# FFN in-projection of a two-layer backbone: products that accumulate in PSUM on copies of other products' sums, and four VectorE combinations a tile instead of seven

## The chip, the core and the metric

One core of one Trainium2 chip runs the whole computation in one launch. The metric is device time in microseconds (us), from the first to the last instruction of the program. The engines are named as in the profile: PE is TensorE (matrix products, from SBUF into PSUM), PEld is its loading of weights, DVE is VectorE, ACT is ScalarE, POOL is GpSimd, SP issues most DMAs. PSUM has eight banks; a bank holds 512 fp32 numbers in each of 128 partitions.

## The reference, cut to what matters

A backbone of two layers works on 512 latent and 256 context tokens with 1024 features. A layer is an FFN, a token mixer (gMLP in layer 0, attention in layer 1), and a second FFN; each has an adaptive shift, scale and gate, and ends in a layer norm.

```python
def swiglu(h, w_in, w_out):
    g, u = jnp.split(h @ w_in, 2, axis=-1)
    return (jax.nn.silu(g) * u) @ w_out

def ffn_sublayer(x, shift, scale, gate, w_in, w_out, ln_g, ln_b):
    y = swiglu(modulate(x, shift, scale), w_in, w_out)
    return layer_norm(ALPHA * x + 0.5 * gate * y, ln_g, ln_b)
```

`w_in` is 1024 x 5632 (2816 columns for g and 2816 for u), everything is fp32. What the change touches is `h @ w_in` with the silu and the product behind it, in three of the four FFNs: the two of layer 0 and the first of layer 1, which all see latent and context tokens (768). The last FFN sees 512 latent tokens and is built otherwise.

## The kernel before, in words

**Precision.** An fp32 operand is held as two parts of type fp32r, hi (a ScalarE copy, `CAST` in the profile) and lo (source minus hi, a VectorE `TENSOR_TENSOR`). A product takes three matmuls: hi x hi, lo x hi, hi x lo.

**A tile of the in-projection.** A tile is 128 of the 2816 columns of g and the same 128 of u, for all 768 tokens: 22 tiles per FFN. The tokens fall into two halves of 384, the 1024 features into two halves of 512. That is a 2 x 2 by 2 x 2 block product (rows: g, u; columns: the two token halves), and it is done by Winograd's form of Strassen's scheme with seven block products instead of eight (`tile_strassen`, line 988). The seven combinations of the input, B11, T1, T2, B21, T3, T4, B22, are `comb` boxes that are made once per FFN; the seven matching combinations of weights are made for each tile. One block product (`product`, line 930) is 4 pieces of 128 features x 3 matmuls = 12 matmuls of 128 x 384 into one bank.

With the products named after the input's combination, in the kernel before:

- g1 = B11 + B21 (second product accumulated in the same bank b1), then silu on ScalarE;
- v = B11, then v += T2; w = v + T3; w += T1; c = v + T3 + T4. T4's product is accumulated on T3's bank b4 and B22's on T1's bank b3 (argument `go_on`), so that one VectorE addition takes both;
- the first token half of the result is silu(g1) x c, the second silu(v + T1 + B22) x w.

This makes seven VectorE operations a tile behind the products: `v+=b2`, `w=v+b4`, `w+=b3`, `c=v+b4`, `g*c`, `v+=b3`, `v*w`. In the profile, `q` (or `pieces`, `acc`, `zraw`) is the SBUF place of v, g, w and c, `ps` a PSUM bank, `stage`, `act` or `acts` where results go for the out-projection.

**The opening.** For the first 8 tiles (`OPENED`) B11 and B21 are run earlier, while the other combinations of the input are still being made (`opening`, `open_half`, `combine`): v (a copy of B11's sum) and g (the silu) then wait in `pieces`, `acc`, `zraw` and so on (`new_pieces`). These opened tiles have five products left, in the order T2, T3, T1, T4, B22. The other 14 have seven: B11, T2, T3, T1, B21, T4, B22.

**The order of the work.** In the openings and in-projections every engine runs its instructions in the order of the Python program (`Pinned`, line 65; `pin`). One product is one slot (`slot`, line 163): the twelve matmuls; then the low halves that are still owed to weights made in the last slot (`flush`); then up to two new weight units (`pump`, from the generator `units`, line 285, which makes the sums and differences of raw weights on VectorE and the hi copies on ScalarE; the low halves are put off to the next flush); then the work behind the product (`post`). So in ScalarE's and VectorE's queues the post of a product stands behind the weights that are made in the same slot. Eight weight units can live at once (`W_BUFS`), two `sums` buffers serve the weight combinations, and while the input's combinations are being made no more than three units are made ahead (`LEAD`).

**Banks.** `bank()` (line 120) takes a tile from one pool of eight buffers with a common tag; the pool decides which of its buffers it is. The gMLP takes its banks from there too: two a chunk for a projection (`project`, each bank 24 matmuls of 128 x 384, read by ScalarE's gelu into `su`), three a chunk for the spatial mixing (`spatial`, 128 x 256 matmuls), and one now and then for a transpose. So do the out-projections, in which six or eight banks collect sums over all weights.

**Places in time** (profiled execution): the in-projections of the three FFNs run from about 40 to 375, 1187 to 1519 and 1697 to 2029 us, where the openings end at about 90, 1230 and 1740; the gMLP's chunks run from 757 to 993 us. `L89` is the line at which `Pinned` issues an instruction, so nearly all instructions of these parts carry it, and they are told apart by the names of their tiles.

Of the kernel before, what the change touches and what calls it, by code (L numbers as in the profile page):

```python
# [13 lines left out]
P = 128  # L14
# [79 lines left out]
class Backbone:  # L94
# [68 lines left out]
    def slot(self, post, n=1, fills=0):  # L163

        self.flush()
        if self.combining is not None:
# [118 lines left out]
    def units(self, jobs):  # L285
        dve, w = self.dve, None
        for kind, srcs in jobs:
# [13 lines left out]
            dve.tensor_tensor(s1, u1, u2, ALU.add)  # L301
            dve.tensor_tensor(s2, s1, g1, ALU.subtract)  # L302
            yield self.unit_of(s2)
# [4 lines left out]
            yield self.unit_of(s1)  # L308
            g2 = self.take()
            if kind == "s":  # L310
                yield self.unit_of(g2)
            w = self.unit_of(u2)
            self.drop(1)
            yield w
            dve.tensor_tensor(s2, g2, s2, ALU.subtract)
            w = self.unit_of(s2)
# [326 lines left out]
    def combine(self):  # L643
# [41 lines left out]
        for name in ("T3", "T4") if begun else ("T3", "T1", "T4"):  # L685
            self.new_comb(name)
        sub(h1[0], h2[0], h1[0])
        sub(h1[1], h2[1], h1[1])
        high("T3", 0, h1[0])
        high("T3", 1, h1[1])  # L690
        yield
        sub(h1[2], h2[2], h1[2])
        high("T3", 2, h1[2])
        low("T3", 0, h1[0])
        if begun:
            low("T3", 1, h1[1])
            high("T4", 0, t4[0])
            yield
            low("T3", 2, h1[2])
            high("T4", 1, t4[1])  # L700
        else:
            high("T1", 0, t1[0])
            yield
            low("T3", 1, h1[1])
            low("T3", 2, h1[2])
            high("T1", 1, t1[1])
            high("T1", 2, t1[2])
# [3 lines left out]
            high("T4", 0, t4[0])  # L711
            high("T4", 1, t4[1])
            yield
            low("T1", 2, t1[2])
        low("T4", 0, t4[0])
        high("T4", 2, t4[2])
        self.new_comb("B22")
        high("B22", 0, h2[0])
# [3 lines left out]
        high("B22", 1, h2[1])  # L722
        high("B22", 2, h2[2])
        yield
        for n in range(HALF):
            low("B22", n, h2[n])
# [1332 lines left out]
```

## Time and profile before

| | |
|---|---|
| three runs | 2817.80, 2817.64, 2816.89 us (median 2817.64) |
| profiled execution, span from first to last instruction | 2816.9 us |
| mean granted TensorE clock | 0.998 |
| PE busy | 2771.2 us (98%), 14478 matmuls |
| DVE busy | 2101.1 us (75%), 3681 instructions |
| ACT busy | 1163.0 us (41%), 2245 instructions |
| POOL busy | 537.4 us (19%) |
| in-projection matmuls `ps<-comb,w` (128 x 384) | 5544, idle before them 9.8 us in all |

How to read the views: a row of the grouped view is "line engine operation out<-in shapes xcount | busy, mean ns | idle time before, and what ended most of it". In a timeline a row is "start, duration, engine, ...", a run of like instructions is drawn together as xN, and [x <-ENGINE tile] is idle time before it and what ended that. A matmul is drawn from its start to its modelled end, and the next one starts before that end. A window's row gives for each engine the busy time and the number of instructions, then the granted clock as a share of the full one, the DMA share and GB/s.

### The profile page before, as it was taken

To read this page: it belongs to the slowest core of one execution; us is meant where nothing else is said; L and a number is where in the kernel's file an instruction comes from. 1 tells how busy PE (TensorE), PEld (TensorE's weight loads), DVE (VectorE), ACT (ScalarE), POOL (GpSimd) and SP (SyncE) were. 2 spreads that over 40 slices of the span, in tenths; PEclk is the share of its full clock that TensorE was granted. 3 is DMA by queue.
4 is the path that set the end of the run, shared out by engine and by line. 5 is a ranking of instruction groups with operands and counts; after the bars stand their busy time and mean duration, and the time that the engine had idled before them with its cause. 6 is when DMAs were issued, how large, how long until landed. Compare 5 with 4: busy or idle time off the path is not lost.

```text
span 2816.9 us, 40812 instructions
## 1 busy us (share of the span) xinstructions
PE 2771.2 (98%) x14478; PEld 2501.4 (89%) x14478; DVE 2101.1 (75%) x3681; ACT 1163.0 (41%) x2245; POOL 537.4 (19%) x605
## 2 busy tenths in 40 slices
PE   7999999999999999999999999999999999999998
PEld 5999988888899988899999889999988888888886
DVE  6988879587687776698888759888886598733445
ACT  6433432442355532463334236333432666623321
POOL 1001044333321232200102220000242121000001
PEclk9999999999999999999999999999999999999999
DMA  7443366366565474344336534434595524454352
GB/s 232 131 135 122 112 225 211 114 199 198 184 180 167 150 237 140 123 148 139 121 121 200 181 113 133 144 120 124 154 314 152 148 69 88 132 150 132 113 168 82
DMA packets 398819, 429.99 MB, mean 153 GB/s; under 512 B 28504, under 2 KB 288024, under 8 KB 398616
## 3 DMA queue, kind: packets, MB, share of 16 engines
q1 hardware_dynamic: 364504, 319.40, 37.0%
q0 software_dynamic: 34112, 108.00, 12.4%
q8 instruction: 113, 1.85, 0.3%
q14 instruction: 90, 0.74, 0.1%
HBM read 366.10 MB, written 63.41 MB: 152 GB/s over the span
## 4 chain that ended last, share of the span: by engine, by line
PE 86%; DVE 5%; issue 3%; ACT 3%; DMA 1%; POOL 1%; SPq 0%; DVEq 0%; POOLq 0%; ACTq 0%
PE ps L89 86%; DVE w L89 1%; DMA raw<-in_w_mod_dram 1%; PE pp L89 1%; POOL acc L383 0%; POOL rs L184 0%; ACT z L1957 0%; DMA raw<-in_ffn_w_in_dram 0%; DVE comb L89 0%; DVE w L156 0%; ACT h L601 0%; ACT p L1473 0%; ACT w L155 0%; ACT w L89 0%; DVE nm L1465 0%
## 5 line engine op out<-in xcount | busy, mean ns | idle before, releaser
L89 PE MATMUL ps<-comb,w 128*128 128x384 f32 x5544 | 972.2, 335 | 9.8 <-DVE q L89 2.6
L89 PEld LDWEIGHTS ps<-comb,w 128*128 128x128 f32 x5544 | 961.1, 188 | 16.8 <-DVE w L89 3.8
L89 PE MATMUL ps<-w,acts 128*128 128x512 f32 (+1 forms) x3792 | 860.1, 388 | 0.0
L89 PEld LDWEIGHTS ps<-w,acts 128*128 128x128 f32 x3792 | 707.3, 188 | 145.0
L89 ACT CAST w<-raw 128x512 fp32r<-128x512 f32 x630 | 387.7, 620 | 819.9 <-PE ps L89 723.2
L89 DVE TENSOR_TENSOR w<-raw,w 128x512 fp32r<-128x512 f32 x630 | 454.8, 729 | 260.0 <-ACT w L89 259.9
L89 PE MATMUL ps<-h,w 128*128 128x384 f32 (+2 forms) x2304 | 445.1, 353 | 0.2 <-DVE w L156 0.2
L89 PEld LDWEIGHTS ps<-h,w 128*128 128x128 f32 x2304 | 402.4, 188 | 37.8 <-DVE w L156 0.4
L89 DVE SCALAR_TENSOR_TENSOR acc<-mraw,cs,acc 128x512 f32<-128x512 f32 x378 | 279.2, 772 | 20.3 <-DMA mraw<-in_w_mod_dram 19.8
L89 PE MATMUL ps<-w,h 128*128 128x512 f32 x1200 | 274.6, 390 | 0.0
L383 POOL PARTITION_ALL_REDUCE acc<-acc x56 | 204.8, 3660 | 351.4 <-DVE acc L89 331.3
L89 PEld LDWEIGHTS ps<-w,h 128*128 128x128 f32 x1200 | 224.6, 188 | 46.3
L89 POOL DMA_DIRECT2D act<-stage x84 | 48.4, 576 | 973.5 <-DVE stage L89 934.6
L89 DVE TENSOR_TENSOR q<-q,ps 128x384 f32<-128x384 f32 (+1 forms) x258 | 143.7, 557 | 106.5 <-PE ps L89 89.3
L89 ACT CAST w<-sums 128x512 fp32r<-128x512 f32 x198 | 122.8, 620 | 237.8 <-DVE sums L302 118.1
L89 POOL DMA_DIRECT2D q<-act x226 | 129.0, 625 | 466.1 <-DVE acts L89 308.4
L89 ACT CAST acts<-q 128x384 fp32r<-128x384 f32 (+1 forms) x262 | 127.3, 519 | 78.9 <-DVE q L89 44.2
L89 DVE TENSOR_TENSOR acts<-q,acts 128x384 fp32r<-128x384 f32 (+1 forms) x262 | 145.5, 588 | 8.3 <-ACT acts L89 8.3
L89 DVE TENSOR_TENSOR w<-sums,w 128x512 fp32r<-128x512 f32 x198 | 140.2, 708 | 1.9 <-ACT w L89 1.9
L156 DVE TENSOR_TENSOR w<-raw,w 128x512 fp32r<-128x512 f32 x114 | 75.8, 688 | 28.8 <-ACT w L155 28.4
L184 POOL TENSOR_TENSOR rs<-ve,mhalf 128x1 f32<-128x1 f32 (+3 forms) x47 | 39.1, 831 | 274.8 <-DVE ve L181 167.7
L155 ACT CAST w<-raw 128x512 fp32r<-128x512 f32 x114 | 68.1, 627 | 48.3 <-PE ps L89 25.5
(203 smaller groups left out, 2162.4 us busy)
## 6 DMA issues: line engine op xcount, KB each, us to landing
raw<-in_ffn_w_in_dram SPq DMA_DIRECT2D x400, 256.0 KB, 3.0
mraw<-in_w_mod_dram SPq DMA_DIRECT2D x256, 256.0 KB, 3.5
raw<-in_ffn_w_out_dram SPq DMA_DIRECT2D x176, 256.0 KB, 3.4
q<-act POOLq DMA_DIRECT2D x216, 192.0 KB, 4.3
act<-stage POOLq DMA_DIRECT2D x74, 384.0 KB, 2.9
raw<-in_gmlp_w_in_dram SPq DMA_DIRECT2D x96, 256.0 KB, 3.3
zhat<-z POOLq DMA_DIRECT2D x26, 512.0 KB, 2.9
raw<-in_gmlp_w_out_dram SPq DMA_DIRECT2D x48, 256.0 KB, 2.9
```

The costliest lines, as they stand in the source:

```text
L89: return self.tc.keep_in_program_order(f(*args, **kwargs))
L155: self.act.copy(hi, src)
L156: self.lows.append((key, lambda: self.dve.tensor_tensor(lo, src, hi.bitcast(F32), ALU.subtract)))
L184: self.last_rstd = self.nc.gpsimd.tensor_tensor(rs, ve, self.mhalf[:, 0:1].to_broadcast([P, n]), ALU.pow).ins
L383: nc.gpsimd.partition_all_reduce(accs[c], accs[c], P, bass_isa.ReduceOp.add)
```

## The change

The matmuls stay the same in number and shape. A block product now accumulates on a bank that already holds what has to be added to it:

- `seeded` is a bank into which ScalarE writes B11's sum: from b1 in a tile with seven products, from v in SBUF in an opened tile. T2's product accumulates on it; ScalarE copies the bank out to v. T3's product accumulates on the same bank; ScalarE copies it out to w. T4's product accumulates on it too, and VectorE multiplies g by the bank itself.
- T1's product goes to bank b2, and ScalarE copies it to p5. B22's product accumulates on b2.
- VectorE is left with four operations: `v += b2`, `w += p5`, `g * seeded`, `v * w`.

The order of the products becomes B11, T1, T2, B21, T3, B22, T4, and T2, T1, T3, B22, T4 in an opened tile. `units` yields the weights in that order, and `combine` makes T1, T3, B22, T4 in that order. `slot` gets `early`, work that stands ahead of the slot's new weights; the seed of a tile with seven products and ScalarE's copies out of T1's, T2's and T3's banks are put there. In an opened tile the seed is copied between the previous tile's last slot and T2's product.

An accumulating matmul on a bank that a copy has written needs a bank that matmuls have already written whole. `bank()` therefore chooses itself among eight tags with one buffer each: the one that was handed out longest ago and isn't held (`hold`, `unhold`), and for `seeded` one whose last user wrote all of the 384 columns (`marked`). This holds for every caller of `bank()` outside the attention, the gMLP included; the out-projections hold their banks until they are read. v and g of opened tile 7 lie in `acc` and no longer in `mraw`.

```diff
-    def bank(self):
-        return self.psum.tile([P, 512], F32, tag="ps", name="ps")
+    def bank(self, hold=None, whole=False, marked=False):
+        if self.pairs:
+            return self.psum.tile([P, 512], F32, tag="ps", name="ps")
+        held = self.bank_held.values()
+        x = next(x for x in self.bank_order if x not in held and (not marked or x in self.bank_whole))
+        self.bank_order.remove(x)
+        self.bank_order.append(x)
...
+        (self.bank_whole.add if whole else self.bank_whole.discard)(x)
+        return self.psum.tile([P, 512], F32, tag=f"ps{x}", bufs=1, name="ps")
...
-    def slot(self, post, n=1, fills=0):
+    def slot(self, post, n=1, fills=0, early=None):
         self.flush()
+        if early:
+            early()
         if self.combining is not None:
...
-        def step(ps, name, post, go_on=False, fills=0):
+        def step(ps, name, go_on, early=None, post=nothing, fills=0):
             self.product(ps, name, go_on)
-            self.slot(post, 2, fills)
+            self.slot(post, 2, fills, early)
             self.release(1)
         add = lambda out, a, b: dve.tensor_tensor(out, a, b, ALU.add)
+        seeded = self.part_bank(marked=True)
         if opened is None:
             b1, v = self.part_bank(), temp()
-            step(b1, "B11", lambda: act.copy(v, b1))
+            step(b1, "B11", False, lambda: act.copy(seeded, b1))
         else:
             v, g = opened
-        b2, b3, b4 = self.part_bank(), self.part_bank(), self.part_bank()
-        step(b2, "T2", lambda: add(v, v, b2))
-        w = temp()
-        step(b4, "T3", lambda: add(w, v, b4), fills=fills)
-        step(b3, "T1", lambda: add(w, w, b3))
+            act.copy(seeded, v)
+        b2, p5, w = self.part_bank(), temp(), temp()
+        keep5 = b2, "T1", False, lambda: act.copy(p5, b2)
+        keep6 = seeded, "T2", True, lambda: act.copy(v, seeded)
         if opened is None:
+            step(*keep5)
+            step(*keep6, fills=fills)
             g = temp()
-            step(b1, "B21", lambda: act.activation(g, b1, AF.Silu), True, int(fills > 1))
-        c = temp()
+            step(b1, "B21", True, None, lambda: act.activation(g, b1, AF.Silu), int(fills > 1))
+        else:
+            step(*keep6)
+            step(*keep5)
+        step(seeded, "T3", True, lambda: act.copy(w, seeded))
+
+        def second():
+            add(v, v, b2)
+            act.activation(v, v, AF.Silu)
+            add(w, w, p5)
+
+        step(b2, "B22", True, None, second)
...
-        def first():
-            add(c, v, b4)
+        def last():
             to = g if m is None else m[:, T1]
-            dve.tensor_tensor(to, g, c, ALU.mult)
+            dve.tensor_tensor(to, g, seeded, ALU.mult)
             done(T1, to)
-
-        step(b4, "T4", first, True)
-
-        def second():
-            add(v, v, b3)
-            act.activation(v, v, AF.Silu)
             to = v if m is None else m[:, T2]
             dve.tensor_tensor(to, v, w, ALU.mult)
             done(T2, to)
-        step(b3, "B22", second, True)
+        step(seeded, "T4", True, None, last)
```

**ScalarE, from one opened tile to the next.** The first rows are ScalarE's queue in the kernel before, in the second FFN, around the silu of its second opened tile (`pieces_11429` is that tile's v; `sums` and `raw` are the sources of weight units).

```order
L89 CAST w_12070<-sums_12067 128x512
L89 CAST w_12088<-raw_11944 128x512
L89 ACTIVATE pieces_11429<-pieces_11429 128x384
L89 CAST w_12114<-sums_12066 128x512
L89 CAST w_12131<-raw_11987 128x512
```

The same place in the changed kernel (`pieces_11415` is v of the second opened tile, `pieces_11477` that of the third, `ps_12079` the third tile's seeded bank):

```order
L89 CAST w_12056<-sums_12053 128x512
L89 ACTIVATE pieces_11415<-pieces_11415 128x384
L89 CAST w_12074<-sums_12052 128x512
L89 COPY ps_12079<-pieces_11477 128x384
L89 COPY pieces_11477<-ps_12079 128x384
L89 CAST w_12099<-raw_11945 128x512
```

The copy into the bank now stands behind the silu and one weight cast of the tile before it; the copy out, behind it, belongs to T2's product.

**VectorE and ScalarE at the first opened tile.** VectorE's queue in the changed kernel, in the second FFN, from the weights that are made in the first tile's T3 and B22 slots to that tile's `v += b2` (`pieces_11415<-pieces_11415,ps_11854`):

```order
L89 TENSOR_TENSOR w_11900<-sums_11894,w_11900 128x512
L339 TENSOR_TENSOR sums_11895<-raw_11828,sums_11895 128x512
L89 TENSOR_TENSOR w_11918<-raw_11758,w_11918 128x512
L320 TENSOR_TENSOR sums_11948<-raw_11877,raw_11920 128x512
L89 TENSOR_TENSOR w_11925<-sums_11895,w_11925 128x512
L89 TENSOR_TENSOR w_11943<-raw_11826,w_11943 128x512
L323 TENSOR_TENSOR sums_11949<-sums_11948,raw_11873 128x512
L89 TENSOR_TENSOR pieces_11415<-pieces_11415,ps_11854 128x384
```

And ScalarE's queue there, from the copy of T3's bank to w (`q_11856<-ps_11852`) to the seed of the second opened tile:

```order
L89 COPY q_11856<-ps_11852 128x384
L89 CAST w_11918<-raw_11758 128x512
L89 CAST w_11925<-sums_11895 128x512
L89 CAST w_11943<-raw_11826 128x512
L89 CAST w_11952<-sums_11949 128x512
L89 ACTIVATE pieces_11415<-pieces_11415 128x384
L89 CAST w_11971<-sums_11948 128x512
L89 COPY ps_11976<-pieces_11415 128x384
```

The addition to v stands behind the weight operations of the seven rows above it on VectorE; the silu that needs it stands behind four casts, and the next seed behind the silu and a cast. (Here the next tile's v is drawn under the same name, since it is another part of the same tile.)

**TensorE in the gMLP.** The matmuls between the projections of the first chunks in the changed kernel; they are the same and in the same order as before, and only the banks differ:

```order
L89 MATMUL ps_7317<-w_sT_7014,vn_7162 128x256 x4
L89 MATMUL ps_7322<-w_sT_7014,vn_7162 128x256 x4
L89 MATMUL ps_7327<-w_sT_7014,vn_7162 128x256 x4
L89 MATMUL ps_7365<-ident_69,s512_7140 128x128
L89 MATMUL ps_7370<-w_sT_7014,vn_7162 128x256 x4
L89 MATMUL ps_7375<-w_sT_7014,vn_7162 128x256 x4
L89 MATMUL ps_7380<-w_sT_7014,vn_7162 128x256 x4
```

Ahead of them stand the four projection banks of chunks 0 and 1, ps_7217, ps_7218, ps_7267 and ps_7268. With the bank that was handed out longest ago, ps_7370, ps_7375 and ps_7380 are the banks of ps_7217, ps_7218 and ps_7267.

More of the change, by code (lines that the diff above doesn't have):

```diff
@@ L684, in combine @@
                 yield
-        for name in ("T3", "T4") if begun else ("T3", "T1", "T4"):
+        for name in ("T3",) if begun else ("T1", "T3"):
             self.new_comb(name)
[L687 to L701, printed above, removed]
+        if not begun:
             high("T1", 0, t1[0])
-            yield
-            low("T3", 1, h1[1])
-            low("T3", 2, h1[2])
             high("T1", 1, t1[1])
-            high("T1", 2, t1[2])
             yield
@@ L721, in combine @@
         low("T4", 2, t4[2])
[L722 to L726, printed above, removed]
     def norm_stats(self, st):
@@ L869, in out_proj_latent @@
                     if not x:
-                        banks[b, half] = self.bank()
+                        banks[b, half] = self.bank(("out", b, half))
                     self.products(banks[b, half], b, [acts.of(order[x])], ws[half : half + 1], x == 0, False)
@@ L974, in new_pieces @@
             self.pieces += [self.zplace()[:, 0:HT] for _ in range(2)]
-        elif f == 7:
-            self.pieces += [
-                self.main.tile([P, 512], F32, tag="mraw", bufs=MRAW_BUFS, name="pieces")[:, 0:HT] for _ in range(2)
-            ]
     def opening(self, seq):
```

81 lines of the change are left out of this document (62 added, 19 removed).

## The prediction

> **What bounds the kernel now.** I read the page's busy times first, then the windows over one in-projection, then TensorE's waits and its timeline at the places where it waited.
>
> ```profile
> span 2816.9 us, 40812 instructions
> ...
> PE 2771.2 (98%) x14478; PEld 2501.4 (89%) x14478; DVE 2101.1 (75%) x3681; ACT 1163.0 (41%) x2245; POOL 537.4 (19%) x605
> ```
>
> TensorE is busy for all but 45.7 us of the span. The columns of the next view are PE, PEld, DVE, ACT, POOL, the granted clock and DMA.
>
> ```profile
> 1225.00:1240.00 15.00, 14.22 (x81) 13.64 (x81) 14.79 (x26) 8.11 (x16) 0.00 (x0) 1.00 0.43 125
> 1240.00:1385.00 145.00, 145.00 (x836) 144.60 (x835) 126.85 (x223) 52.59 (x93) 7.60 (x14) 1.00 0.45 137
> 1385.00:1400.00 15.00, 14.52 (x84) 14.20 (x83) 14.66 (x19) 5.18 (x10) 9.03 (x5) 1.00 0.34 96
> ```
>
> In the long window of the third sublayer's in-projection TensorE has no idle time: 145.00 us for 836 matmuls is 173.4 ns each, 2.08 us for a product of 12. The change leaves that number of matmuls alone, so VectorE work saved there is worth nothing by itself. VectorE is full (14.79 of 15, 14.66 of 15) only at the first tile and near one later tile. What it costs TensorE there is in its waits, cut here to the time from 60 to 2030 us:
>
> ```profile
> PE ps L89 <- DVE q L89: 2.6, 5, 0.5
> ...
> PE ps L89 <- ACT w L89: 1.4, 3, 0.9
> ```
>
> ```profile
> 79.75 11.89 PE L89 MATMUL ps<-comb,w 128*128 128x384 f32 x66
> 92.51 2.32 PE L89 MATMUL ps<-comb,w 128*128 128x384 f32 x12 [0.87 <-ACT w L89]
> 95.38 104.86 PE L89 MATMUL ps<-comb,w 128*128 128x384 f32 x603 [0.55 <-DVE q L89]
> ```
>
> ```profile
> 1208.78 27.32 PE L89 MATMUL ps<-comb,w 128*128 128x384 f32 x156
> 1236.33 1.97 PE L89 MATMUL ps<-comb,w 128*128 128x384 f32 x10 [0.23 <-ACT w L89]
> ```
>
> ```profile
> 1236.33 2.33 PE L89 MATMUL ps<-comb,w 128*128 128x384 f32 x12 [0.23 <-ACT w L89]
> ...
> 1398.50 1.68 PE L89 MATMUL ps<-comb,w 128*128 128x384 f32 x8 [0.48 <-DVE q L89]
> ```
>
> ```profile
> L89 PE MATMUL ps<-comb,w 128*128 128x384 f32 x5544 | 972.2, 335 | 9.8 <-DVE q L89 2.6 <-DVE w L89 2.6 <-ACT w L155 2.3
> ```
>
> A matmul's end is shown 335 ns after its start while the next is due after 173, so an idle time of x is a delay of x + 0.16. The 12 matmuls behind a wait take 2.33 us, not 12 x 0.1734 + 0.16 = 2.24: 0.09 more. The eight waits of the first view come to 2.6 + 1.4 + 8 x 0.25 = 6.0 us. Another 0.4 us goes at 83.04, where a product waits for ScalarE's late copy out of its bank.
>
> ```profile
> 83.04 8.27 PEld L89 LDWEIGHTS ps<-comb,w 128*128 128x128 f32 x48 [0.33 <-ACT pieces L89]
> ```
>
> So **6.4 us is all that relieving VectorE can give back.** The waits of "DVE w" lie in the openings, whose weights do not change.
>
> **The change, part by part.**
>
> *Matmuls and combinations.* 7 products a tile before and after. Three of seven combinations go, 3 x 66 x 0.55 us = 109 us of VectorE, which lies beside a TensorE that never pauses, but for those 6.4 us.
>
> ```profile
> L89 DVE TENSOR_TENSOR q<-q,ps 128x384 f32<-128x384 f32 x246 | 135.4, 551 | 57.3 <-PE ps L89 40.1 <-ACT w L89 12.2
> ```
>
> ```profile
> L89 ACT CAST acts<-q 128x384 fp32r<-128x384 f32 x240 | 114.0, 510 | 77.4 <-DVE q L89 44.1 <-DMA q<-act 32.8
> ...
> L89 ACT ACTIVATE q<-q 128x384 f32<-128x384 f32 x45 | 23.7, 526 | 88.0 <-DVE q L89 88.0
> ...
> L89 ACT COPY q<-ps 128x384 f32<-128x384 f32 x44 | 21.0, 478 | 10.4 <-PE ps L89 10.4
> ```
>
> *ScalarE copies.* The three that empty T1's, T2's and T3's banks take 0.48 us each, and one product (2.08 us) stands between each and the matmul that needs the bank. That product hides them; without it each would hold TensorE some 0.6 us. In the 14 unopened tiles the seed is copied after B11 with T1 in between: hidden too. No copy from SBUF into PSUM is in the trace; it lies between 0.48 (out of PSUM) and 0.53 (SBUF to SBUF). I take 0.51, the row that also reads SBUF.
>
> The Trainium skill (PSUM — Partial Sum Buffer, Specifications) says that ScalarE writes PSUM faster than SBUF; no row here shows it. With 0.48 for a seed the sum below would be 0.6 us smaller.
>
> *The seed of the opened tiles* is the wait that the change adds: v already lies in SBUF, and T2, which accumulates on the seed, directly follows the previous tile's T4. On ScalarE the seed stands behind that tile's silu and a weight cast, and the silu behind VectorE's v + B22. The rows of one tile now, where B22 is the last product and the addition was released by TensorE:
>
> ```profile
> 1813.79 0.55 DVE L89 TENSOR_TENSOR zraw<-zraw,ps 128x384 f32<-128x384 f32 x1 [0.33 <-PE ps L89]
> 1814.37 0.53 ACT L89 ACTIVATE zraw<-zraw 128x384 f32<-128x384 f32 x1 [2.00 <-DVE zraw L89]
> 1814.81 0.61 ACT L89 CAST w<-raw 128x512 fp32r<-128x512 f32 x1
> ```
>
> ```profile
> 1235.62 0.61 ACT L89 CAST w<-raw 128x512 fp32r<-128x512 f32 x1
> ...
> 1236.14 0.61 ACT L89 CAST w<-sums 128x512 fp32r<-128x512 f32 x1
> ```
>
> From the addition's start: silu at 0.58, cast at 1.02, next ScalarE instruction 0.52 later (second fence) at 1.54, seed done at 2.05, TensorE 0.10 after that (the cast of 1235.62 ends at 1236.23, the matmul starts at 1236.33): 2.15. T2 is due 12 matmuls after T4 started, and T4 started 0.20 before the addition: 1.88. So 0.27 + 0.09 = **0.36 us for a tile that follows an opened one**, from 0.1 (a short seed, a quick start) to 0.6 (the addition held up). In a third of the tiles it now starts up to 0.1 later, but then VectorE had more to do. There are 7 such places in each of 3 sublayers. At 18 of them, 6.5 us; the first of each is worse.
>
> *The first opened tile.* Its seed stands behind the opening's last silu. In the second FFN (1200 to 1519 us), T2 was due three products before 1236.10 - 0.16, at 1229.70. The last opening product ends at 1229.86, silu 0.04 later, the next ScalarE instruction 0.38 on (half of the row below), seed 0.51, start 0.10: 1230.89, so 1.2 + 0.09 = 1.3 us. The first FFN has a comb cast in between (0.52): 1.8 + 0.09 = 1.9. Bounds 1.0 and 2.5 each: ScalarE was at most some tenths late there.
>
> *The step from the first to the second opened tile.* Two weights a slot are still made ahead there. I walk the new order with 0.60 us for a 512-wide VectorE operation (two in 1.28 below), 0.52 for a cast, 0.04 from one engine to the next, t = 0 at T2's start; the products end at 2.33, 4.41, 6.49, 8.57.
>
> ```profile
> 1215.33 1.28 DVE L89 TENSOR_TENSOR z<-z 128x512 f32<-128x512 f32 x2
> ```
>
> ScalarE copies T2 at 2.4 and casts B22's and T4's weights at 2.7 and 3.3; VectorE's low halves of these follow at 3.4 and 4.0, the next tile's s2 at 4.6. ScalarE casts it and s1 at 5.3 and 5.9, copies T3 at 6.5, casts u1 at 6.9. VectorE: two low halves and g2 - s2, 6.0 to 7.9, cast at 7.9 and 8.45 with u2; then u1's low half, an s1, two low halves and an s2, 7.8 to 10.9. **Only then comes v + B22, at 10.8, though B22's sum was there at 8.6.** ScalarE casts that s2 at 10.9; silu 11.45, cast 11.9, seed 12.4 to 12.9, T2 at 13.0, due at 10.49: 2.5 + 0.09 = 2.6 us. The third FFN has the same order. In the first, a further cast stands ahead of the silu and one behind it; the two behind wait for sums that VectorE makes only after the addition, so the same walk gives T2 at 14.0, 3.6 us. Bounds 1.5 and 4.0. In the second tile one weight a slot is made, the addition is free by 8.6, and the 0.36 holds.
>
> *Banks in the gMLP.* bank() now takes the bank that was handed out longest ago, also there. The third mixing bank of chunk 1 is the eighth after the first half of chunk 1's projection, which ScalarE has not yet read. TensorE reaches it after 8 of the 12 matmuls of 774.76, at 775.9; the gelu that frees it runs at 776.98.
>
> ```profile
> 774.76 1.91 PE L89 MATMUL ps<-w_sT,vn 128*128 128x256 f32 x12
> ```
>
> ```profile
> 776.98 0.87 ACT L89 ACTIVATE su<-ps 128x384 f32<-128x384 f32 x2
> ```
>
> It ends at 777.47: 0.10 later TensorE goes on, 1.6 + 0.09 = 1.7 us, once; from nothing (ScalarE earlier) to 2.5.
>
> *The rest:* holds in the out-projections hand banks out in the order of before; T4's combination comes later, but its low halves are through before the tile's T4; tile 7's acc places are free before the first fill of tile 8. Nothing.
>
> **The sum.** First FFN 1.9 + 3.6 + 6 x 0.36 = 7.7; second and third 1.3 + 2.6 + 2.2 = 6.1 each; gMLP 1.7: 21.6 us of new waits, less the 6.4 that go: +15.2. On the profiled span 2816.9, which lies 0.7 under the median 2817.64 of the runs, that is 2832.1; I say **2832 us, slower by 0.5%**. With all terms at their low ends 1.8 + 4.5 + 3.0 - 6.4 = +2.9, at the high ones 10.8 + 12 + 7.5 + 2.5 - 5 = +28.
>
> **The rivals.**
>
> *Hidden seeds.* If ScalarE reaches the steady seeds in time, because PSUM is nearer or the addition starts sooner, their 6.5 us go: 2826. For it: only 0.27 us are missing. Against: every hop is a row. 12%.
>
> *All of the cover holds (the other side).* VectorE's relief also pulls in the first two seeds and the gelu; nothing is left but the eight waits and the late copy: 2816.9 - 6.4 = 2810.5, faster by 0.2%. It decides if the first tile's silu runs before the casts of the next weights. For it: VectorE is full just there. Against: the casts stand ahead of it in the order. 4%.
>
> *A balance.* Weights are ready earlier than walked, the first steps cost 1.5 and no bank waits: 3 x 1.5 + 4.5 + 18 x 0.2 - 6.4 = +6 at most, 2817 to 2823: 8%.
>
> *The clock falls.* TensorE pauses 2.6 and 3.6 us in one piece, longer than any wait in the FFNs now. Early in the kernel the clock did fall, after a broken stretch, and not after a wait of 1.89 us:
>
> ```profile
> 30.00:40.00 10.00, 6.53 (x40) 4.09 (x38) 7.67 (x20) 6.79 (x13) 0.00 (x0) 1.00 0.97 312
> 40.00:50.00 10.00, 9.30 (x56) 7.35 (x56) 6.44 (x13) 8.39 (x21) 0.00 (x0) 0.83 0.67 208
> 50.00:60.00 10.00, 8.00 (x46) 7.14 (x46) 7.91 (x17) 8.16 (x17) 0.00 (x0) 1.00 0.81 226
> ```
>
> ```profile
> 40.70 3.76 PE L89 MATMUL ps<-comb,w 128*128 128x384 f32 x12
> ...
> 51.51 0.62 PE L89 MATMUL ps<-comb,w 128*128 128x384 f32 x2 [1.89 <-ACT w L155]
> ```
>
> The product at 40.70 took 3.76 instead of 2.24. Three times 1.5 us: 2832 + 4.6 = 2837. 12%.
>
> The Trainium skill (TensorE: Matmul & The Clock Gate, What's actually happening) puts the drop behind an idle window of about 3.4 us; by that rule only the wait in the first FFN could reach it, 2833.5. The 1.89 us without a drop agree.
>
> **How the numbers follow.** Forecast 64%, its own range 2826 to 2838 from the bounds of the first steps and the seeds; the rivals 12, 4, 8 and 12%. The range 2823 to 2840 leaves out the fast side, most of the balance, and a few per cent above. Slower by over 0.2% (some 5.6 us, about what a measurement can tell from no change): forecast, hidden seeds and falling clock, 88%; within it the balance, 8%; faster 4%.
>
> **What would show it.** In the profile after, TensorE's waits in the FFNs name ScalarE's writes into ps (a COPY ps<-pieces and its like), some 24 of them: 18 near 0.1 to 0.3 us of idle time, one of 2 to 3.5 us in each FFN a tile after the opening, one of 1 to 2 us at its end. The waits for "DVE q" and "ACT w" near 92, 1236 and 1398 are gone, VectorE is some 100 us less busy, ScalarE as much more. A wait of TensorE for gelu stands near 785. No wait at the opened tiles would make the seeds' chain wrong; waits of 1 us there would say that the addition is held up in every tile; a TensorE whose matmul spacing changes would make all of it wrong.

## The result

The changed kernel takes **2835.75 us** (median of 4 runs, 2835.25 to 2836.71) where the kernel before took 2817.72 (4 runs, 2816.89 to 2818.25): ratio **1.0064**, 95% interval 1.0050 to 1.0079. It is slower by 18.0 us; 2832 with 2823 to 2840 was forecast.

The profile of the changed kernel, with the lines that answer to those shown of before: its page (span, busy time of the engines),

```profile
span 2834.9 us, 40738 instructions
...
PE 2781.4 (98%) x14478; PEld 2508.5 (88%) x14478; DVE 2012.9 (71%) x3483; ACT 1245.0 (44%) x2467; POOL 537.6 (19%) x605
```

TensorE's waits from 60 to 2050 us (engine and tile that wait, engine and tile that end the wait; us in all, times, longest),

```profile
PE ps L89 <- ACT ps L89: 12.6, 6, 3.3
PE ps L89 <- DVE w L89: 2.5, 4, 0.7
PE ps L89 <- ACT su L89: 1.4, 1, 1.4
```

and its timeline at the first tiles of the first and the second FFN:

```profile
85.03 10.70 PE L89 MATMUL ps<-comb,w 128*128 128x384 f32 x60 [1.73 <-ACT ps L89]
99.00 11.20 PE L89 MATMUL ps<-comb,w 128*128 128x384 f32 x48 [3.27 <-ACT ps L89]
```

```profile
1238.53 10.69 PE L89 MATMUL ps<-comb,w 128*128 128x384 f32 x60 [1.19 <-ACT ps L89]
1251.85 78.41 PE L89 MATMUL ps<-comb,w 128*128 128x384 f32 x432 [2.63 <-ACT ps L89]
```

VectorE is 88 us less busy (some 100 was forecast), ScalarE 82 more, and the waits for "DVE q" and "ACT w" are gone. In their place stand six long waits for a seed, two in each FFN. The 18 short ones lie below what the first view lists: their idle time is 0.01 each, but the start of the matmul comes 0.17 late and the next one 0.11.

To see where the 18 us came from, I compared the start of the same matmul in the two traces, stage by stage:

| part | after minus before, us |
|---|---|
| start of the program, to 70 us | -1.8 |
| first FFN's in-projection | +7.9 |
| gMLP, chunk 1 | +1.4 |
| in-projection at 1200 to 1519 us | +5.5 |
| in-projection at 1710 to 2029 us | +5.5 |
| the rest | -0.4 |
| sum | 18.1 |

The start of the program differs by up to 3.2 us between the profiled executions of all kernels below, the change's -1.8 among them, so I compare places in the traces behind it rather than single times (of the experiments only `seed_early` and `best` have more than one run). Behind it the change is 19.9 us later, the seeds, the clock and the bank together, less what VectorE's relief gives back.

### The profile page after: what moved, and what is told of

It reads as the page before. It is cut to its first block, busy times and chain, and to the rows that moved or that the text cites. A ratio compares the mean times of both kernels' runs of the same rounds, so it can differ in the third digit from the quotient of the medians.

```text
span 2834.9 us, 40738 instructions
## 1 busy us (share of the span) xinstructions
PE 2781.4 (98%) x14478; PEld 2508.5 (88%) x14478; DVE 2012.9 (71%) x3483; ACT 1245.0 (44%) x2467; POOL 537.6 (19%) x605
## 4 chain that ended last, share of the span: by engine, by line
PE 63%; ACT 3%; DVE 3%; issue 2%; POOL 1%; DMA 0%; DVEq 0%; POOLq 0%; ACTq 0%; SPq 0%
PE ps L89 62%; PE pp L89 1%; POOL acc L410 0%; ACT z L1991 0%; DVE z L89 0%; POOL rs L203 0%; ACT h L628 0%; DVE comb L89 0%; ACT w L89 0%; ACT p L1507 0%; DVE w L89 0%; DMA raw<-in_ffn_w_in_dram 0%; DVE nm L1499 0%; ACT w L172 0%; ACT comb L642 0%
## 5 line engine op out<-in xcount | busy, mean ns | idle before, releaser
L89 PE MATMUL ps<-comb,w 128*128 128x384 f32 x5544 | 982.8, 337 | 17.6 <-ACT ps L89 12.6
L89 PEld LDWEIGHTS ps<-comb,w 128*128 128x128 f32 x5544 | 967.8, 189 | 28.2 <-ACT ps L89 20.7
L89 PE MATMUL ps<-w,acts 128*128 128x512 f32 (+1 forms) x3792 | 860.1, 388 | 0.0
L89 PEld LDWEIGHTS ps<-w,acts 128*128 128x128 f32 x3792 | 707.6, 188 | 144.7
L89 ACT CAST w<-raw 128x512 fp32r<-128x512 f32 x630 | 388.2, 621 | 743.4 <-PE ps L89 651.4
L89 DVE TENSOR_TENSOR w<-raw,w 128x512 fp32r<-128x512 f32 x630 | 456.1, 732 | 321.4 <-ACT w L89 321.0
L89 PE MATMUL ps<-h,w 128*128 128x384 f32 (+2 forms) x2304 | 445.1, 353 | 0.2 <-DVE w L173 0.2
L89 PEld LDWEIGHTS ps<-h,w 128*128 128x128 f32 x2304 | 402.4, 188 | 37.7 <-DVE w L173 0.4
L89 DVE SCALAR_TENSOR_TENSOR acc<-mraw,cs,acc 128x512 f32<-128x512 f32 x378 | 279.3, 772 | 20.9 <-DMA mraw<-in_w_mod_dram 20.6
L89 PE MATMUL ps<-w,h 128*128 128x512 f32 x1200 | 274.6, 390 | 0.0
L89 PEld LDWEIGHTS ps<-w,h 128*128 128x128 f32 x1200 | 224.7, 188 | 46.3
L89 POOL DMA_DIRECT2D act<-stage x84 | 48.3, 575 | 1004.3 <-DVE stage L89 975.2
L89 POOL DMA_DIRECT2D q<-act x226 | 128.6, 620 | 455.1 <-DVE acts L89 311.7
L89 DVE TENSOR_TENSOR w<-sums,w 128x512 fp32r<-128x512 f32 x198 | 135.8, 687 | 81.7 <-ACT w L89 81.5
L89 ACT COPY q<-ps 128x384 f32<-128x384 f32 x179 | 85.8, 479 | 213.0 <-PE ps L89 209.7
L89 DVE TENSOR_TENSOR acts<-q,acts 128x384 fp32r<-128x384 f32 (+1 forms) x262 | 149.2, 606 | 12.0 <-ACT acts L89 11.9
L89 ACT CAST acts<-q 128x384 fp32r<-128x384 f32 (+1 forms) x262 | 126.6, 519 | 52.5 <-DMA q<-act 37.0
L89 ACT CAST w<-sums 128x512 fp32r<-128x512 f32 x198 | 122.8, 622 | 24.2 <-DVE sums L339 13.1
```

Source lines behind the costliest of these rows:

```text
L89: return self.tc.keep_in_program_order(f(*args, **kwargs))
```

## The experiments

**Is it VectorE's load that made TensorE wait before?** `relief_alone` changes the kernel before:

```diff
-        step(b2, "T2", lambda: add(v, v, b2))
-        w = temp()
-        step(b4, "T3", lambda: add(w, v, b4), fills=fills)
-        step(b3, "T1", lambda: add(w, w, b3))
+        step(b2, "T2", lambda: None)
+        w = v
+        step(b4, "T3", lambda: None, fills=fills)
+        step(b3, "T1", lambda: None)
```

> The kernel before, with three of VectorE's seven combinations a tile left out (v += b2, w = v + b4 and w += b3; v takes the place of w, so the output isn't the reference's), and all matmuls, their order and the banks as they were. Theory (the eight waits of TensorE of 0.23 to 0.87 us at the first tiles and near two later ones come from VectorE's load): they go, the span falls by 5 to 6.4 us below that of before outside the first 70 us. Rival (they come from the order of the weights and combinations there, not from the load): at least the waits at the first tiles, 4.5 us of the 6.4, stay.

Measured: 2811.74 us (one run; before on that chip 2819.08). TensorE's waits from 60 to 2030 us are down to one row, that of the openings:

```profile
PE ps L89 <- DVE w L89: 2.6, 4, 0.7
```

The eight waits are gone: 5.96 us in the traces at their places (1.9, 1.3, 0.76, 1.3, 0.76). ScalarE's late copy at 83 us, 0.28 us, stayed, so that one wasn't VectorE's. At five of the eight ("DVE q") the matmul waited for one of the additions that are left out here. So this run shows what those additions and their lateness cost, and not yet that the load alone brings waits.

`relief_undone` goes the other way: three VectorE additions a tile more, in a kernel that had no waits left at these tiles (`seed_early`, below).

```diff
+        more = lambda a: add(d, a, v)
-            step(*keep6, fills=fills)
+            step(*keep6, post=lambda: more(v), fills=fills)
...
-        step(seeded, "T3", True, lambda: act.copy(w, seeded))
+        step(seeded, "T3", True, lambda: act.copy(w, seeded), lambda: more(d))
...
+            more(d)
             to = g if m is None else m[:, T1]
```

> The kernel with the early seeds, and three more VectorE additions of 128x384 a tile (into a place that nobody reads) behind T2, T3 and T4, so that VectorE has as many operations as before. Theory (load): waits of TensorE for VectorE of 0.2 to 0.9 us come back at the first tiles and near one later tile of an FFN, 3 to 7 us in all. Rival (order): none come back, under 1 us.

Measured: 2819.45 us, 5.8 us more than `seed_early` behind the start. Two rows of TensorE's timeline, near the first tiles and at the first FFN's last tile:

```profile
100.17 2.38 PE L89 MATMUL ps<-comb,w 128*128 128x384 f32 x12 [0.83 <-ACT pieces L89]
...
365.52 4.80 PE L89 MATMUL ps<-comb,w 128*128 128x384 f32 x26 [1.57 <-ACT ps L89]
```

They name ScalarE, since TensorE now waits for copies, but all that was added is VectorE work. So VectorE's load does make TensorE wait. That both totals are near 6 us is in part chance: 2.1, 0.6 and 0.6 us came back at the first tiles of the three FFNs, and 1.6, 0.6 and 0.3 at their last tiles, where the kernel before had no wait.

**Is it the seed's place in ScalarE's queue?** `seed_early` copies the seed of the next opened tile one slot earlier:

```diff
         for n, (f, half) in enumerate(seq):
-            self.slot(self.open_half(f, half), 2)
+            self.slot(self.open_half(f, half), 2, early=self.seed_next if n == len(seq) - 1 else None)
...
+    def seed_next(self):
+        if self.begun:
+            self.seeded = self.part_bank(marked=True)
+            self.act.copy(self.seeded, self.begun[min(self.begun)][0])
...
             v, g = opened
-            act.copy(seeded, v)
...
-        step(b2, "B22", True, None, second)
+        step(b2, "B22", True, self.seed_next, second)
```

> The changed kernel with one thing moved: the seed of the next opened tile is copied in the B22 slot of the tile before (the first tile's in the opening's last slot), ahead of that slot's weights and silu. Theory (the place in the queue): the copies cost nothing by themselves; the three first seeds (1.73, 1.19, 1.19 us of idle time), the three steps to the second tile (3.27, 2.63, 2.58), the 18 steady waits (0.01 each, 0.28 with the broken spacing) and the slow matmuls behind the three long ones all go: 2835.75 less 24.5 gives 2811, within 2809 to 2813. Rival 1 (the copy itself: a matmul that accumulates on a bank that ScalarE wrote has to wait for it wherever it stands): the 18 steady waits of 0.28 stay, 2816. Rival 2 (the weights are late at the second tile too): the waits of 2.6 to 3.3 stay there under the name of a weight, 2823 or more.

Measured: 2814.76 us (10 runs) against 2818.90 for the kernel before on that chip, ratio 0.9985, interval 0.9975 to 0.9994. In the trace it is 23.9 us ahead of the changed kernel behind the start, where 24.5 was expected. ScalarE's timeline from the first to the second opened tile shows the seed (`ps<-pieces` at 1238.83) ahead of the silu, which is as late as in the changed kernel (11.8 us after the first tile's T2 starts, at 1230.28):

```profile
1238.83 0.48 ACT L89 COPY ps<-pieces 128x384 f32<-128x384 f32 x1
1239.24 0.62 ACT L89 CAST w<-raw 128x512 fp32r<-128x512 f32 x1
1241.59 0.62 ACT L89 CAST w<-sums 128x512 fp32r<-128x512 f32 x1 [1.73 <-DVE sums L323]
1242.11 0.52 ACT L89 ACTIVATE pieces<-pieces 128x384 f32<-128x384 f32 x1
```

and TensorE runs 684 matmuls behind one wait of 0.28:

```profile
1230.28 118.86 PE L89 MATMUL ps<-comb,w 128*128 128x384 f32 x684 [0.28 <-ACT ps L89]
```

So accumulating on a bank that ScalarE wrote cost TensorE nothing here once the copy was done in time, and the weights of the second tile were in time. Both rivals fall.

**What holds the seed at the second tile?** The working of the prediction put it on the addition v + B22, behind a slot's weights on VectorE. `second_early` moves that addition, its silu and w + p5 ahead of those weights, in the first opened tile alone:

```diff
-        step(b2, "B22", True, None, second)
+        if len(self.begun) == OPENED - 1:
+            step(b2, "B22", True, second)
+        else:
+            step(b2, "B22", True, None, second)
```

> The changed kernel with v + b2, its silu and w + p5 of the first opened tile alone put ahead of the weights of its B22 slot; all else as it was. Theory (VectorE reaches the addition late because it stands behind that slot's weights): the addition starts within 0.9 us of B22's last matmul instead of 2.7, the wait before the second tile falls from 3.27, 2.63 and 2.58 to under 0.7 us in each FFN, the matmuls behind it keep their spacing, and the three first seeds (1.73, 1.19, 1.19) stay: 2835.75 less 14.5 plus at most 3 x 0.6 gives 2821 to 2823. Rival (all of the first tile's weights are late, and with them whatever stands behind): the waits stay over 2 us, 2831 or more.

Measured: 2836.88 us, nothing gained. The waits are 3.27, 2.42 and 2.54 us, so this expectation was wrong. TensorE's second tile, and VectorE and ScalarE from the addition to that tile's seed:

```profile
1253.49 2.70 PE L89 MATMUL ps<-comb,w 128*128 128x384 f32 x14 [2.42 <-ACT ps L89]
```

```profile
1250.27 0.55 DVE L89 TENSOR_TENSOR pieces<-pieces,ps 128x384 f32<-128x384 f32 x1
...
1251.20 0.69 DVE L323 TENSOR_TENSOR sums<-sums,raw 128x512 f32<-128x512 f32 x1
```

```profile
1250.85 0.52 ACT L89 ACTIVATE pieces<-pieces 128x384 f32<-128x384 f32 x1 [1.84 <-DVE pieces L89]
1251.28 0.60 ACT L89 CAST w<-raw 128x512 fp32r<-128x512 f32 x1
1251.92 1.14 ACT L89 CAST w<-sums 128x512 fp32r<-128x512 f32 x2
1252.96 0.47 ACT L89 COPY ps<-pieces 128x384 f32<-128x384 f32 x1
```

The addition did come earlier, 9.90 us after T2's first matmul (1240.37) instead of 11.22. But the weight work then stood behind it, and the seed behind two casts that wait for a sum of VectorE (L323, done at 1251.89). VectorE has hardly a gap from 1246.45 on: whichever of its operations comes first, the seed stands behind VectorE's work. (Behind the start this trace is 2.7 us ahead of the changed kernel's, nearly all of it in fewer slow matmuls behind the waits; see the clock below.)

That says the amount of work is the cause. `one_weight` makes one weight instead of two in each slot of the opened tiles:

```diff
-            self.slot(post, 2, fills, early)
+            self.slot(post, 2 if opened is None else 1, fills, early)
```

> The changed kernel with one new weight instead of two in each slot of the opened tiles; seeds, products and posts stand as they did. With the addition alone moved ahead the wait before the second tile stayed at 2.4 to 3.3 us, since VectorE was busy without a gap from the second slot on and the seed then stood behind casts that waited for VectorE. Theory (it is the amount of weight work made in the first tile, 12 VectorE operations of 0.6 us before the addition, now 7, that makes the seed late): VectorE reaches the addition as soon as B22's product is there, and the wait before the second tile falls to the steady 0.3 us lost, or at most 0.8, in all three FFNs, with no slow matmuls behind; the three first seeds stay: 2835.75 - 14.5 + 1 to 2 = 2822 to 2824. Rival (other work than the weights made ahead holds the seed there): the waits stay over 2 us, 2832 or more.

Measured: 2828.25 us (before, one run: 2816.71). TensorE's timeline in the second FFN, from the first opened tile to the third:

```profile
1234.36 10.70 PE L89 MATMUL ps<-comb,w 128*128 128x384 f32 x60 [1.18 <-ACT ps L89]
1245.35 10.70 PE L89 MATMUL ps<-comb,w 128*128 128x384 f32 x60 [0.29 <-ACT ps L89]
1256.33 5.84 PE L89 MATMUL ps<-comb,w 128*128 128x384 f32 x32 [0.29 <-ACT ps L89]
```

The wait before the second tile is 0.29 us in all three FFNs: the theory holds. The total is 5 us over what I expected, because the 18 later tiles now wait 0.29 too instead of 0.01 (18 x 0.28 = 5.0 us more): with one weight a slot, a weight sum (L339) comes to stand on VectorE just ahead of the addition.

**Would a product between help?** `t1_first` puts T1 ahead of T2 in the opened tiles, and their weights in that order (the weights' part of the edit is not shown):

```diff
-            step(*keep6)
-            step(*keep5)
+            step(*keep5)
+            step(*keep6)
```

> The changed kernel with T1 ahead of T2 in the opened tiles (and their weights in that order), so that one product of 2.08 us lies between the tile before and the product that needs the seed. Theory (the seed is late by a fixed time after the tile before): the first seeds and the 18 steady waits go, since they are late by less than 2.08; at the second tile 3.43 - 2.08 = 1.4 us stays in the first FFN and 0.7 in the other two, and after waits this short the matmuls keep their spacing: 2835.75 - 4.9 - 5.0 - 11.5 = 2814, within 2812 to 2817. Rival (VectorE and ScalarE are behind by more than a product at the opened tiles): waits of over 1 us stay in all three FFNs, 2820 or more.

Measured: 2840.39 us, and 1.2 us behind the change in the traces behind the start: nothing gained. The seed waits did what was expected (1.35 us in the first FFN, 0.63 in the others, no slow matmuls). But I had overlooked what the new order does to T2: T3 now follows it directly on the same bank, and has to wait for ScalarE's copy of it.

```profile
100.57 2.35 PE L89 MATMUL ps<-comb,w 128*128 128x384 f32 x12 [1.35 <-ACT ps L89]
103.55 10.70 PE L89 MATMUL ps<-comb,w 128*128 128x384 f32 x60 [0.62 <-ACT pieces L89]
114.87 10.70 PE L89 MATMUL ps<-comb,w 128*128 128x384 f32 x60 [0.62 <-ACT pieces L89]
```

That is the price of a copy out of a bank that no product hides: 0.62 us of idle time, 0.9 lost with the delayed starts, 24 times.

**The gMLP.** `gmlp_banks` holds a projection's banks until their gelu is issued, and hands them out first after it (`True`: to the front of the order):

```diff
-            banks = [self.part_bank(), self.part_bank()]
+            banks = [self.part_bank(("u", n, x)) for x in range(2)]
...
                 act.activation(u[:, cols], ps, AF.Gelu)
+                self.unhold(("u", j, x), True)
```

> The changed kernel with the gMLP's projection banks held until their gelu is issued, and then handed out first. Theory (the wait before the third mixing product of chunk 1 is for the bank alone): the 1.38 us before it go, nothing else moves by over 0.3, 2835.75 - 1.4 = 2834.4. Rival (ScalarE is late there for another reason, and the next matmul waits instead): the same 1.4 us stand before the next bank that a gelu frees, 2835.7.

Measured: 2835.16 us; in the trace 1.39 us less at chunk 1 and nothing elsewhere in the gMLP. The twelve mixing matmuls of chunk 1 run through:

```profile
780.95 1.91 PE L89 MATMUL ps<-w_sT,vn 128*128 128x256 f32 x12
```

**The clock.** Behind the waits at the second tile the matmuls came 0.32 us apart instead of 0.173. The granted clock of a trace changes only at times that are multiples of 3.41 us apart; cut along these edges, the windows of the changed kernel around two of the waits (PE busy, granted clock, DMA) are:

```profile
94.48:97.89 3.41, 1.25 (x8) 1.00 0.56 160
97.89:101.31 3.42, 2.31 (x7) 0.50 0.44 159
101.31:104.72 3.41, 3.41 (x12) 0.50 0.54 153
104.72:108.13 3.41, 3.41 (x21) 1.00 0.26 77
1248.17:1251.59 3.42, 1.04 (x6) 1.00 0.69 203
1251.59:1255.00 3.41, 3.15 (x10) 0.50 0.37 125
1255.00:1258.41 3.41, 3.41 (x21) 1.00 0.51 147
```

A window in which TensorE is busy for only 1.25 or 1.04 us is followed by one at half the clock. A window at half the clock with 2.31 us of work is followed by another (97.89), one with 3.15 us is not (1251.59). `pauses` puts pauses of graded length into `seed_early`, in 18 tiles:

```diff
+PAUSES = [0, 0, 3, 4, 5, 6, 7, 8, 0, 0, 9, 10, 12, 4, 5, 6, 0, 0, 7, 8, 9, 10, 12, 14]
...
             v, g = opened
+            for _ in range(PAUSES.pop(0)):
+                act.copy(seeded, v)
```

> The kernel with the early seeds, in which TensorE waits for nothing at the opened tiles, and in the third to eighth tile of each FFN the seed copied again n times just before T2 (n = 3, 4, 5, 6, 7, 8 in the first FFN, 9, 10, 12, 4, 5, 6 in the second, 7, 8, 9, 10, 12, 14 in the third). A copy follows a copy after 0.38 us, so TensorE pauses 0.38 (n - 1) us: 0.8 to 4.9. The pauses cost 18 x 0.28 + 0.38 x (139 - 18) = 51 us. Theory (the granted clock falls after a pause of over about 2 us, between 1.73, behind which matmuls kept 0.173 us, and 2.58, behind which they came 0.32 apart): slow matmuls behind the pauses of n = 8 and more in every case (9 of 18), with n = 6 and 7 to be seen, none with n = 3 to 5; with 1.5 to 2.5 us each 2814.8 + 51 + 18 = 2884. Rival, by the Trainium skill (TensorE: Matmul & The Clock Gate, What's actually happening), that an idle window of about 3.4 us is needed: only n = 10 and more (5 of 18), 2876. Second rival (it is not the length of the pause alone, but how it falls on windows of the clock's control): pauses of one length fall on both sides.

Measured: 2907.68 us. A further copy costs 0.51 us, not 0.38, so the pauses are 1.55 to 6.70 us. No slow matmul follows pauses of 1.55 (twice), 2.08, 2.24, 2.58 (twice) and 3.10; slow ones follow 2.07, 3.61 (twice), and all seven from 4.1 to 5.7, and 6.70: 11 of 18. TensorE's timeline at pauses that stand against each other (L90 is the L89 of the other kernels):

```profile
160.36 10.70 PE L90 MATMUL ps<-comb,w 128*128 128x384 f32 x60 [3.10 <-ACT ps L90]
```

```profile
1335.89 12.24 PE L90 MATMUL ps<-comb,w 128*128 128x384 f32 x60 [2.07 <-ACT ps L90]
1350.71 5.50 PE L90 MATMUL ps<-comb,w 128*128 128x384 f32 x30 [2.58 <-ACT ps L90]
```

So the length alone does not decide, as the second rival has it. In windows of 3.41 us (PE, PEld, DVE, ACT and POOL busy, granted clock, DMA) it comes out in order:

```profile
155.38:158.79 3.41, 1.88 (x11) 1.56 (x9) 3.38 (x7) 2.87 (x7) 0.00 (x1) 1.00 0.36 108
158.79:162.20 3.41, 1.84 (x10) 1.85 (x11) 1.69 (x3) 1.45 (x3) 0.54 (x1) 1.00 0.54 188
...
1332.98:1336.39 3.41, 1.34 (x8) 1.02 (x7) 3.33 (x6) 2.72 (x6) 0.55 (x1) 1.00 0.47 138
1336.39:1339.80 3.41, 3.41 (x12) 3.41 (x11) 0.69 (x1) 0.02 (x1) 0.00 (x0) 0.50 0.33 127
1346.62:1350.04 3.42, 1.51 (x9) 1.19 (x7) 2.71 (x6) 3.24 (x7) 0.54 (x1) 1.00 0.51 150
1350.04:1353.45 3.41, 2.74 (x15) 2.74 (x16) 1.39 (x2) 0.85 (x3) 0.00 (x0) 1.00 0.30 118
```

The pause of 3.10 falls on two windows, each with over 1.8 us of work, and the clock stays; that of 2.07 falls whole into one, which has 1.34 us of work, and the next is slow. Over all windows of the eleven traces (before, the change and the nine experiments, from 60 to 2250 us), every one at full clock with 1.91 us of idle time or less was followed by full clock, and every one with 2.07 or more by half of it. The wait of 2.42 in `second_early` belongs here too: it falls on two windows, neither with less than 1.9 us of work, and no slow matmul stands behind it (the edges of these rows are 0.04 us off that trace's grid; PE, PEld, DVE, ACT and POOL as above).

```profile
1248.60:1252.01 3.41, 2.47 (x15) 2.15 (x13) 3.31 (x7) 1.53 (x4) 0.00 (x0) 1.00 0.52 154
1252.01:1255.42 3.41, 1.93 (x11) 1.93 (x12) 3.41 (x7) 1.43 (x3) 0.49 (x1) 1.00 0.47 135
```

In the first 60 us idle time does not sort the windows so well: some with 1.46 to 1.9 us of it were followed by half the clock (the change's at 29.62, with 1.51), one with 1.64 was not (`relief_undone` at 24.14). There the matmuls come in many short runs, and a matmul's modelled end, 335 ns behind its start where the next is due after 173, hides a part of every pause. What exactly is counted stays open.

**A version that beats both.** `best` joins `seed_early`, with the first tile's seed one slot earlier still, and `gmlp_banks`:

```diff
-            self.slot(self.open_half(f, half), 2, early=self.seed_next if n == len(seq) - 1 else None)
+            self.slot(self.open_half(f, half), 2, early=self.seed_next if n == len(seq) - 2 else None)
```

> The kernel with the early seeds, the first tile's seed one slot earlier still, and the gMLP's projection banks held until their gelu and handed out first. The first seed's 0.28 us in the second and third FFN go (0.55 each with the broken spacing), and 1.4 in the gMLP: 2814.8 - 2.5 = 2812.3, that is 6.6 us under the kernel before on the same chip, ratio 0.9977. Rival (the earlier seed or the held banks make TensorE wait elsewhere): 0.9985 or more.

Measured: **2811.43 us** (8 runs, 2810.95 to 2812.29) against 2819.08 for the kernel before on that chip (12 runs): ratio **0.9971**, interval 0.9960 to 0.9981. The windows of the second FFN's in-projection that began the prediction now read:

```profile
1225.00:1240.00 15.00, 15.00 (x88) 15.00 (x87) 14.08 (x24) 10.20 (x22) 0.00 (x0) 1.00 0.45 134
1240.00:1385.00 145.00, 145.00 (x838) 144.71 (x836) 109.41 (x188) 68.64 (x137) 7.61 (x14) 1.00 0.47 139
1385.00:1400.00 15.00, 15.00 (x88) 15.00 (x88) 13.20 (x16) 5.53 (x11) 7.08 (x3) 1.00 0.34 97
```

TensorE has no gap in any of the three. Freeing VectorE was worth its 6 us; what the change lost were the seeds' place, the clock behind them, and one bank.

## Why the prediction was right, and where it was not

| term | predicted, us | measured, us |
|---|---|---|
| relief of VectorE | -6.4 | -6.4 (5.96 at the eight waits) |
| first seed, first FFN / others | 1.9 / 1.3 | 2.0 / 1.5 |
| second tile, first FFN / others | 3.6 / 2.6 | 3.5 / 2.9 |
| 18 steady seeds | 18 x 0.36 = 6.5 | 18 x 0.28 = 5.0 |
| bank in the gMLP | 1.7 | 1.4 |
| slow matmuls behind the long waits | 0 (a rival: 4.6) | 5.7 |

A measured wait is its idle time plus the 0.16 and 0.1 of the delayed starts; the slow matmuls are counted apart (2.6, 1.5 and 1.6 us over a spacing of 0.1734; 16, 8 and 9 of the starts came late by 0.15 us, the one ahead of them by 0.31). With the rest (-0.4, and 0.25 at one tile, below) the measured terms come to the 19.9 us of the traces behind the start. The forecast was +15.2. It was set on the profiled span of 2816.9; times lie 1.8 us above spans (2836.71 and 2834.9 in the change's profiled run), so the sum belonged on the median, 2817.64, and gives 2832.8.

**The bound: right.** TensorE's matmuls kept their number and, but for those behind the three long waits, their spacing. What VectorE's relief gave back was the eight waits: the change and `relief_alone` are both 5.96 us ahead of the kernel before at their places.

**The first seeds: right.** The 0.38 us from the silu to the seed in the second FFN is what the trace has (1237.60 to 1237.98), though it is not half of the 0.87 that was cited for it.

**The steady seeds: right in place and cause, some 30% too long.** The hops of one tile in the second FFN, on ScalarE:

```profile
1273.24 0.53 ACT L89 ACTIVATE pieces<-pieces 128x384 f32<-128x384 f32 x1 [1.15 <-DVE pieces L89]
1273.67 0.61 ACT L89 CAST w<-sums 128x512 fp32r<-128x512 f32 x1
1274.18 0.47 ACT L89 COPY ps<-pieces 128x384 f32<-128x384 f32 x1
```

With the addition's start at 1272.65 these are 0.59, 1.02 and 1.53, as walked; then the seed took 0.47 instead of 0.51, and TensorE started at 2.06 instead of 2.15. No copy from SBUF into PSUM was in the trace of before; its group here (last), that of the seeds from B11's bank and that of the copies out of the banks are

```profile
L89 ACT COPY q<-ps 128x384 f32<-128x384 f32 x179 | 85.8, 479 | 213.0 <-PE ps L89 209.7 <-DVE w L89 3.3
L89 ACT COPY ps<-ps 128x384 f32<-128x384 f32 x42 | 19.5, 463 | 74.4 <-PE ps L89 74.3
...
L89 ACT COPY ps<-pieces 128x384 f32<-128x384 f32 x12 | 5.7, 478 | 0.0
```

so of the two rows that bounded it, the other end (0.48) was the right one. The Trainium skill (PSUM — Partial Sum Buffer, Specifications) has ScalarE write faster to PSUM than to SBUF. The same copy out of PSUM took 463 ns into PSUM and 479 into SBUF, which agrees, by 16 ns; the 0.51 and 0.53 from SBUF to SBUF belong to other operations, a cast and a silu.

**The second tile: right in size, incomplete in cause.** The walk gave the addition at 10.8 us after T2's start and the next T2 at 13.0; measured were 11.2 and 13.3. But "only then comes v + B22" named one operation where `second_early` shows that its place doesn't matter: the seed stands behind a VectorE that is full. `one_weight`, with less work, and `seed_early`, with the seed ahead of that work, each took the wait away.

**The clock: the wrong case was put first.** The step that failed is "Early in the kernel the clock did fall, after a broken stretch, and not after a wait of 1.89 us", from which I gave a fall behind the 2.6 and 3.6 us only 12%. All three long waits had slow matmuls behind them, 5.7 us, as that rival had it. Without them the traces behind the start would differ by 14.2 us, 1.0 less than forecast. With them the time lies 3.75 above the 2832, near the 2837 of that rival: the total stayed in the range since the range had room for a term that the working had put at nothing. By the forecast's own sign, a matmul spacing that changes, it failed at these three places and held everywhere else. What the step missed is that the length of a wait does not decide, but how it falls on the windows, as `pauses` shows. The rule of the Trainium skill (TensorE: Matmul & The Clock Gate, What's actually happening), an idle window of about 3.4 us, would have spared the two waits of 2.6 us; in the trace the clock fell behind them too. The same section has windows that run freely, of 3413 ns, and there the traces agree: every two changes are a multiple of 3.41 us apart.

**The gMLP's bank: right**, as `gmlp_banks` shows, 0.3 us shorter since ScalarE reached that gelu 0.2 us earlier.

**"The rest: nothing"** was right but for 0.25 us at the first FFN's last tile, where a seed stands behind casts that wait for VectorE.

**The other rivals.** Hidden seeds, full cover and the balance did not come about; that full cover was near is shown by `best`, which reaches it by moving the seeds.

## What to carry to other kernels

A copy that only has to be ready early belongs in the queue where its inputs are ready, not where its consumer stands in the program: behind work that waits for another engine it inherits that engine's lateness, and changing the order among that engine's operations does not help while it is full. On a matmul-bound kernel a pause of TensorE can cost more than its length: under the windows seen here (60 to 2250 us), pauses that leave a window of 3.41 us with less than about 1.4 us of work cost a further 1.3 to 2.8 us. When a buffer pool's rule is changed for one stage, look at every other stage that draws from it.

## What the runs showed of the hardware that was not expected

In these traces the granted clock changed only on a fixed grid of 3.41 us. From 60 to 2250 us a window at full clock with 2.07 us of idle time or more was followed by one at half clock, one with 1.91 or less never, whatever the length of the pause; in the first 60 us that line does not hold. From 60 to 2250 us, too, a window at half clock with 0.77 us of idle time or more was followed by another (`pauses`), and one with 0.55 or less ended the slow stretch (`gmlp_banks` at 99.78). The wait of 1.89 us at 51.51 in the kernel before, which I had taken as evidence of a longer threshold, lies across an edge of that grid at 50.64 (its slow window begins at 40.40, and 50.64 is three windows on), so neither window had 1.9 us of idle time from it.
